# Second-half key and query projections beside the banded attention, value and gate projections in the first DeltaNet phase, and filler work ranked first

## The chip, the cores and the metric

One NeuronCore of a Trainium2 chip runs the whole kernel. The metric is the device time of one execution in microseconds (us), the median of several runs. PE is TensorE (its weight loads are PEld), DVE is VectorE, ACT is ScalarE, POOL is GpSimd, SP is SyncE, whose queue issues most loads from DRAM.

## What is computed

One encoder layer, applied with the same weights to two sequences: a prompt of 512 rows and a sample of 256, each row 1024 wide, all in float32. Tokens are held as six tiles of 128 rows (0 to 3 prompt, 4 and 5 sample).

```python
def _layer(x, mem, ...):
    h = _rms_norm(x, g_pre_mix)
    proj = h @ w_in
    att = _window_attention(aq, ak, av, attn_sink)      # 8 heads, 2 key/value heads, blocks of 128, sink
    dn = _deltanet(qkv, z, ...)                         # 4 heads of 128, conv of 5 taps, both directions
    mix = jnp.concatenate([att, dn], -1) @ w_out
    x = x + _rms_norm(mix, g_post_mix)
    h = _rms_norm(x, g_pre_xa)
    x = x + _rms_norm(_cross_attention(h, mem, xa_wq, xa_wkv, xa_wo, mem_g), g_post_xa)
    h = _rms_norm(x, g_pre_mlp)
    x = x + _rms_norm(jnp.square(jax.nn.relu(h @ w1)) @ w2, g_post_mlp)
    return x
```

The gated DeltaNet takes queries, keys and values through a convolution over time and a SiLU, solves a triangular system in each chunk of tokens, and scans the chunks forward and backward; its output is normed and multiplied by the SiLU of the gate z. The cross-attention's keys and values come from 256 memory rows for each sequence (`mn @ wkv`, 512 columns of keys, 512 of values).

## The kernel before

**Products.** Every large float32 product is made of three matmuls on rounded halves: an operand x becomes hi, a rounded copy made by ACT, and lo, the rest x - hi made by DVE or POOL; hi*hi, hi*lo and lo*hi are added up in PSUM (`mm3`, lines 186 to 190).

**Weights.** `Weights` (lines 82 to 114) holds the units in the order in which they are planned. `get(key, ahead)` calls `emit`, which issues, up to some units ahead of the one wanted, a load on SP into a `raw` tile (line 107; two buffers), the ACT copy to hi (line 108) and the subtraction to lo (line 109). In the first part hi and lo have four buffers each. Which engine subtracts is a function of the key (line 207): POOL for the attention's weights and for the first-half DeltaNet blocks, DVE for the rest.

**What orders the work.** The kernel is traced by generators. `run` and `chain` go through them one after another, `merge` takes steps from two in a given ratio. The framework then writes each engine's instruction order at build time: an instruction that was traced earlier ranks higher, and a later one is put ahead where, by the framework's own timing, the earlier ones are not ready. So a generator that is chained behind another is filler for it. On the chip each engine keeps to its written order. Tiles of one tag share that tag's buffers, in traced order.

**Stages.** `run` (line 193) first norms and transposes the rows and projects the attention's heads (`proj_first`, `proj_att`). Then `merge` interleaves the banded attention (`window`, weight 150) with `proj_dn` for half 0, that is heads 0 and 1 (weight 48, line 220). `proj_dn` (line 539) makes keys, queries and values (kinds 1, 0, 2) of two heads each: six blocks. A block is `feature_major` (line 495): 8 steps of three pairs of matmuls, 512 columns (line 505) and 256 (line 506), into two PSUM banks of one tag; then ACT copies the banks into a padded buffer (lines 549, 550), the convolution runs as one ACT and four DVE steps (lines 554 to 557), a tanh and a DVE product follow, and six transposes (line 568).

Then two DeltaNet phases run, one for each half (`deltanet`, line 658). Each has `prep` (Gram matrices, decays), `inverse`, whose loop of small dependent DVE products (lines 735 and 739) inverts 32-row blocks and is followed by block products on PE, and a scan over the token tiles (`step`). Behind the first phase stands `proj_dn` for half 1 (six blocks), behind the second `fill` (line 276): two of the four memory tiles (`memory_prep`), gate blocks z 0 to 2 (`proj_z`), two more memory tiles, z 3, and the memory's keys and values (`memory_kv`, eight blocks of 128 columns; the four value blocks are transposed afterwards, line 408).

`memory_prep` squares and scales a memory tile on ACT, transposes it in two halves of four, through the tags `tr` (one bank) and `mm` (two banks), and writes hi on ACT (line 388) and lo on DVE (line 389). hi lies in the buffer of half 0's keys, queries and values, so it can be written only when the first phase has read them. The memory rows have two buffers.

Then `tail` makes the output projection, the cross-attention and, while these last, the first part of the MLP for the sample tiles (`up`, line 265, one bank); the MLP follows.

## Time and profile before

| | |
|---|---|
| median of 3 runs | 1214.59 us (1214.43 to 1216.47) |
| profiled execution, its own time | 1215.08 us |
| its span, first to last instruction | 1213.3 us |
| PE busy in the span | 1120.0 us, 92% |
| DVE, ACT, POOL busy | 708.1, 529.4, 355.5 us |
| mean granted TensorE clock | 0.963 of 2.4 GHz |

Times in the profile count from the span's start. A row of waits names the line and tile that waited, then what released it. In the clock column 1.00 is 2.4 GHz and 0.50 is 1.2 GHz. By the timeline the banded attention runs from 94 to 223, the first DeltaNet phase from 223 to 347 (prep to 250, loop to 283, block products to 304, scan), the second from there to 449 (prep to 362, loop to 387, block products to 413, scan), the rest of the memory's keys and values to 497, the tail to about 720.

### The profile page before, as it was taken

The numbers are of one execution on the slowest core, as the hardware profiler recorded it, in microseconds if no ns is written. First come the engines' busy times: TensorE is split into PE (matmuls) and PEld (weight loads), VectorE is DVE, ScalarE is ACT, GpSimd is POOL, SyncE is SP. The second block draws the span as 40 slices with busy tenths as digits, with TensorE's granted clock in tenths as the row PEclk, the third lists the DMA queues.
The fourth block names the chain that finished last, engine by engine and source line by source line (L and its number), as shares of the span: only waits on it lengthen the run. The fifth ranks groups of instructions, "written<-read, shape, count | busy, mean of one in ns | idle before, by whom it ended". The sixth has DMA issues, their size and how long they took to land.

```text
span 1213.3 us, 17783 instructions
## 1 busy us (share of the span) xinstructions
PE 1120.0 (92%) x6800; PEld 958.7 (79%) x6800; DVE 708.1 (58%) x1263; ACT 529.4 (44%) x1119; POOL 355.5 (29%) x415
## 2 busy tenths in 40 slices
PE   6998999976959998899899989999999999999995
PEld 5887888865857887678787778888888888888884
DVE  5313455799789452455535646365658565658656
ACT  5336767755474333433434534443233332333322
POOL 5353210011111020011100136353536353526461
PEclk9999999988989698899899999999999999999998
DMA  6355311211312028732622233122212222212114
GB/s 199 98 180 160 94 53 37 78 35 36 75 48 92 28 93 253 239 122 82 231 70 70 88 122 96 43 75 65 88 53 76 63 70 70 87 52 61 44 57 169
DMA packets 108703, 113.81 MB, mean 94 GB/s; under 512 B 10079, under 2 KB 81867, under 8 KB 108619
## 3 DMA queue, kind: packets, MB, share of 16 engines
q1 hardware_dynamic: 100971, 99.55, 27.3%
q10 hardware_dynamic: 7648, 13.13, 2.9%
q8 instruction: 53, 0.87, 0.3%
q14 instruction: 31, 0.25, 0.1%
HBM read 91.27 MB, written 21.39 MB: 93 GB/s over the span
## 4 chain that ended last, share of the span: by engine, by line
PE 42%; issue 3%; POOL 2%; DVE 2%; DMA 1%; ACT 1%; POOLq 0%; DVEq 0%; ACTq 0%
PE up L1195 7%; PE up L1196 7%; PE up L1197 7%; PE y L189 5%; PE y L188 5%; PE y L190 5%; POOL y L1257 1%; DMA raw<-in_xa_wo 1%; PE xa L1156 1%; PE xa L1137 1%; PE mm L1121 1%; PE mm L1120 1%; PE mm L1119 1%; POOL rs L153 1%; PE mm L188 0%
## 5 line engine op out<-in xcount | busy, mean ns | idle before, releaser
L1200 POOL TENSOR_TENSOR hid<-hid 128x256 f32<-128x256 f32 (+1 forms) x64 | 61.1, 955 | 220.3 <-ACT hid L1199 220.3
L190 PE MATMUL y<-w,hl 128*128 128x512 f32 x318 | 123.8, 389 | 0.5 <-DVE hl L184 0.5
L189 PE MATMUL y<-w,hh 128*128 128x512 f32 x318 | 123.7, 389 | 0.0
L188 PE MATMUL y<-w,hh 128*128 128x512 f32 x318 | 123.7, 389 | 0.0
L1239 DVE TENSOR_TENSOR y<-y,y 128x512 f32<-128x512 f32 x72 | 48.9, 683 | 106.8 <-PE y L190 106.8
L1199 ACT ACTIVATE hid<-up 128x256 f32<-128x256 f32 (+1 forms) x64 | 31.2, 488 | 174.3 <-PE up L1197 174.3
L1195 PE MATMUL up<-hx0h,w 128*128 128x512 f32 x256 | 100.0, 390 | 1.0 <-DVE hx0l L184 1.0
L1196 PE MATMUL up<-hx0l,w 128*128 128x512 f32 x256 | 99.9, 390 | 0.0
L1197 PE MATMUL up<-hx0h,w 128*128 128x512 f32 x256 | 99.6, 389 | 0.0
L109 DVE TENSOR_TENSOR w<-raw,w 128x1024 fp32r<-128x1024 f32 (+1 forms) x58 | 78.8, 1365 | 31.4 <-ACT w L108 31.4
L997 POOL TENSOR_TENSOR quad<-quad 128x1024 f32<-128x1024 f32 x28 | 77.7, 2774 | 33.8 <-DVE w L109 20.2
L109 DVE TENSOR_TENSOR w<-quad,w 128x1024 fp32r<-128x1024 f32 x49 | 73.2, 1505 | 11.9 <-ACT w L108 11.9
L1195 PE MATMUL up<-hx4h,w 128*128 128x256 f32 x256 | 72.2, 282 | 4.2 <-ACT hid L1199 4.2
L1196 PE MATMUL up<-hx4l,w 128*128 128x256 f32 x256 | 71.7, 280 | 0.1
L1197 PE MATMUL up<-hx4h,w 128*128 128x256 f32 x256 | 71.4, 279 | 0.0
L108 ACT ACTIVATE w<-raw 128x1024 fp32r<-128x1024 f32 (+1 forms) x58 | 55.3, 963 | 35.7 <-DMA raw<-in_w_out 11.0
L190 PEld LDWEIGHTS y<-w,hl 128*128 128x128 f32 x318 | 59.7, 188 | 13.3 <-DVE hl L184 0.9
L189 PEld LDWEIGHTS y<-w,hh 128*128 128x128 f32 x318 | 59.7, 188 | 12.4
L188 PEld LDWEIGHTS y<-w,hh 128*128 128x128 f32 x318 | 59.7, 188 | 12.4
L183 ACT ACTIVATE hh<-hid 128x768 fp32r<-128x768 f32 x37 | 31.4, 848 | 83.2 <-PE y L189 64.0
L184 DVE TENSOR_TENSOR hl<-hid,hh 128x768 fp32r<-128x768 f32 x37 | 43.0, 1162 | 24.8 <-ACT hh L183 24.6
L1195 PEld LDWEIGHTS up<-hx0h,w 128*128 128x128 f32 x256 | 48.1, 188 | 10.4 <-DVE hx0l L184 1.2
(373 smaller groups left out, 3114.5 us busy)
## 6 DMA issues: line engine op xcount, KB each, us to landing
raw<-in_mlp_w SPq DMA_DIRECT2D x36, 512.0 KB, 4.5
quad<-in_mlp_w SPq DMA_DIRECT2D x28, 512.0 KB, 4.6
raw<-in_w_in SPq DMA_DIRECT2D x44, 256.0 KB, 3.0
d_x<-x ACTq DMA_DIRECT2D x12, 512.0 KB, 2.6
x<-d_x SPq DMA_DIRECT2D x12, 512.0 KB, 3.7
x<-in_x_prompt SPq DMA_DIRECT2D x8, 512.0 KB, 4.0
raw<-in_xa_wkv SPq DMA_DIRECT2D x16, 256.0 KB, 3.2
d_att<-parts SPq DMA_DIRECT2D x12, 256.0 KB, 2.0
```

The lines of the kernel that those rows point to most:

```text
L108: self.nc.scalar.activation(hi[:, c], raw, AF.Copy)
L109: self.sub(key)(out=lo[:, c], in0=raw, in1=hi[:, c].bitcast(F32), op=ALU.subtract)
L184: nc.vector.tensor_tensor(out=lo, in0=src, in1=hi.bitcast(F32), op=ALU.subtract)
L188: nc.tensor.matmul(ps, lh, rh, start=first, stop=False)
L189: nc.tensor.matmul(ps, lh, rl, start=False, stop=False)
L190: nc.tensor.matmul(ps, ll, rh, start=False, stop=last)
L997: nc.gpsimd.tensor_tensor(out=out, in0=x, in1=y, op=ALU.subtract)
L1195: nc.tensor.matmul(ps, wh[:, k], hh[:, k], start=k == 0, stop=False)
L1196: nc.tensor.matmul(ps, wh[:, k], hl[:, k], start=False, stop=False)
L1197: nc.tensor.matmul(ps, wl[:, k], hh[:, k], start=False, stop=k == 7)
L1200: nc.gpsimd.tensor_tensor(out=r, in0=r, in1=r, op=ALU.mult)
L1239: nc.vector.tensor_tensor(out=y, in0=y, in1=ps, op=ALU.add)
```

## The change

The half-1 keys and queries are chained behind half 0's six blocks and interleaved with the attention (weight 80 for 48). `proj_dn` for half 1 behind the first phase has values alone, and the four z blocks follow it. `fill` keeps `memory_prep` and `memory_kv`. The memory's values are made with the memory rows as the stationary operand, eight units of 128 rows by 512 columns into four banks at once, so they need no transposes. The low parts of half 1's keys and queries go to POOL. `emit`, the transposes and writes of `memory_prep`, and ACT's copies of finished banks in `proj_dn` and `proj_z` are traced inside `high_priority()`, which ranks them ahead of everything else. The first `up` takes the tags `up` and `mm` in turn.

```diff
 class Weights:
     def emit(self, upto):
+        with self.tc.high_priority():
+            self.emit_now(upto)
+
+    def emit_now(self, upto):
         while self.n < min(upto, len(self.q)):
...
 def run(self):
-                         (wp, 512, 2), lambda key: self.nc.gpsimd if key[0] in ("att", "ba") or key[0] == "dn" and key[2] < 2 else self.nc.vector)
+                         (wp, 512, 2), lambda key: self.nc.gpsimd if key[0] in ("att", "ba") or key[0] == "dn" and (key[2] < 2 or key[1] < 2) else self.nc.vector)
...
-        run(merge((self.proj_dn(cv, 0, keep0, ("mm", "dnp")), 48), (self.window(at), 150)))
+        early = chain(self.proj_dn(cv, 0, keep0, ("mm", "dnp")), self.proj_dn(cv, 1, keep1, ("mm", "dnp"), (1, 0)))
+        run(merge((early, 80), (self.window(at), 150)))
...
-        run(self.deltanet(dn, 0, keep0), self.proj_dn(cv, 1, keep1, ("mm", "wn")))
+        run(self.deltanet(dn, 0, keep0), self.proj_dn(cv, 1, keep1, ("mm", "wn"), (2,)), *(self.proj_z(cv, h) for h in range(4)))
...
-        self.up(0, 4, first, "up", 0)
+        self.up(0, 4, first, ("up", "mm"), 0)
...
 def fill(self, pool, m0, keep):
-        prep = self.memory_prep(m0, hh, hl)
-        next(prep)
-        next(prep)
-        yield from self.proj_z(pool, 0)
-        yield from self.proj_z(pool, 1)
-        yield from self.proj_z(pool, 2)
-        next(prep)
-        next(prep)
-        yield from self.proj_z(pool, 3)
+        yield from self.memory_prep(m0, hh, hl)
         yield from self.memory_kv(pool, hh, hl)
...
 def plan_m(self):
-        for m in range(8):
+        for m in range(4):
             for k in range(2):
                 self.W.plan(("kv", m, k), wkv[:, 4 * k:4 * k + 4, m * P:(m + 1) * P], 4, P)
+        for k in range(8):
+            self.W.plan(("v", k), wkv[:, k:k + 1, 512:1024], 1, 512)
...
 def memory_prep(self, m0, hh, hl):
             nc.scalar.activation(x, x, AF.Copy, scale=r)
+            hp = self.tc.high_priority()
+            hp.__enter__()
             for b in (0, 4):
...
+            hp.__exit__(None, None, None)
             yield
...
 def memory_kv(self, pool, hh, hl):
-        for m in range(8):
+        for m in range(4):
...
-            if m < 4:
-                nc.scalar.dma_start(self.d_kT[m], t)
-            else:
-                pt = self.ps("tr")
-                for i in range(4):
-                    nc.tensor.transpose(pt[:, i * P:(i + 1) * P], t[:, i * P:(i + 1) * P], self.ident)
-                v = pool.tile([P, 770], F32, tag="tanh", bufs=1, name="kvv")[:, :512].rearrange("p (i d) -> p i d", i=4)
-                nc.scalar.activation(v, pt.rearrange("p (i d) -> p i d", i=4), AF.Copy)
-                c = (m - 4) * P
-                nc.scalar.dma_start(self.d_v[:, :, c:c + P].rearrange("i p d -> p i d"), v)
+            nc.scalar.dma_start(self.d_kT[m], t)
+
+        pv = [self.ps(("mm", "wn")[i % 2], "mv") for i in range(4)]
+        for k in range(8):
+            wh, wl = self.W.get(("v", k), 3)
+            for i in range(4):
+                c = slice(i * P, (i + 1) * P)
+                self.mm3(pv[i], hh[:, k, c], hl[k // 4][:, k % 4, c], wh[:, 0], wl[:, 0], k == 0, k == 7)
+                yield
+        for i in range(4):
+            v = pool.tile([P, 770], F32, tag="y", bufs=2, name="kvv")[:, :512]
+            nc.scalar.activation(v, pv[i], AF.Copy)
+            nc.scalar.dma_start(self.d_v[i], v)
...
 def proj_z(self, pool, h):
-            nc.scalar.activation(z[:, c], ps, AF.Copy)
+            with self.tc.high_priority():
+                nc.scalar.activation(z[:, c], ps, AF.Copy)
...
-    def proj_dn(self, pool, half, keep, tags):
+    def proj_dn(self, pool, half, keep, tags, kinds=(1, 0, 2)):
-        for kind in (1, 0, 2):
+        for kind in kinds:
...
-                nc.scalar.activation(xp[:, 2:514], pp, AF.Copy)
-                nc.scalar.activation(xp[:, 516:772], psa, AF.Copy)
+                with self.tc.high_priority():
+                    nc.scalar.activation(xp[:, 2:514], pp, AF.Copy)
+                    nc.scalar.activation(xp[:, 516:772], psa, AF.Copy)
...
 def up(self, b, s0, R, tag, ahead=3, ms=range(4)):
-            ps = self.ps(tag, "up")[:, :n]
+            ps = self.ps(tag if isinstance(tag, str) else tag[m % len(tag)], "up")[:, :n]
```

## Rows read from the trace of the kernel before

**Rows 1.** The page, part 1: busy us (share of span) xcount.

```profile
PE 1120.0 (92%) x6800; PEld 958.7 (79%) x6800; DVE 708.1 (58%) x1263; ACT 529.4 (44%) x1119; POOL 355.5 (29%) x415
```

**Rows 2.** Windows by stage: length, busy us (x) of engines, PEclk, DMA.

```profile
94.00:223.00 129.00, 122.34 (x838) 107.33 (x838) 64.85 (x168) 88.86 (x229) 22.99 (x35) 0.99 0.27 77
223.00:250.00 27.00, 22.01 (x139) 19.39 (x137) 21.79 (x47) 18.84 (x47) 0.00 (x0) 1.00 0.30 79
250.00:283.00 33.00, 22.42 (x112) 18.79 (x113) 32.28 (x126) 13.46 (x41) 8.61 (x7) 0.82 0.14 35
283.00:304.00 21.00, 19.92 (x377) 16.31 (x377) 19.50 (x28) 15.05 (x36) 2.33 (x4) 0.88 0.18 48
304.00:347.00 43.00, 40.70 (x313) 36.50 (x308) 32.01 (x88) 20.62 (x70) 9.15 (x18) 1.00 0.29 72
347.00:362.00 15.00, 5.80 (x38) 4.85 (x38) 13.93 (x28) 14.78 (x39) 0.26 (x2) 0.81 0.14 42
362.00:387.00 25.00, 21.39 (x112) 18.13 (x113) 23.62 (x121) 10.79 (x24) 1.43 (x3) 0.84 0.29 91
387.00:413.00 26.00, 23.45 (x364) 19.41 (x362) 16.61 (x32) 13.46 (x29) 2.32 (x4) 0.70 0.13 42
413.00:449.00 36.00, 35.46 (x255) 32.09 (x255) 18.30 (x56) 12.14 (x34) 5.98 (x12) 0.93 0.17 56
449.00:497.00 48.00, 41.74 (x177) 33.01 (x176) 14.43 (x23) 18.91 (x38) 2.03 (x4) 0.92 0.76 231
```

**Rows 3.** Waits of PE from 223 to 497: us in total, times, longest.

```profile
PE mm L505 <- DVE wlo L109: 15.2, 2, 8.5
PE tp L384 <- DVE hm L389: 12.2, 1, 12.2
```

**Rows 4.** Timeline of PE near 365: start, us, operation [idle before <-releaser].

```profile
365.19 1.11 PE L384 MATMUL tp<-ident,xm 128*128 128x128 f32 x4 [12.25 <-DVE hm L389]
...
370.06 0.39 PE L505 MATMUL mm<-hh,whi 128*128 128x512 f32 x1
...
371.10 0.39 PE L505 MATMUL mm<-hh,whi 128*128 128x512 f32 x1
```

**Rows 5.** Windows of line 505: length, PE busy (x), PEld busy (x), PEclk, DMA.

```profile
0.00:94.00 94.00, 5.40 (x15) 2.81 (x15) 1.00 0.51 161
94.00:223.00 129.00, 55.61 (x143) 27.44 (x143) 0.99 0.27 77
```

**Rows 6.** Groups of DVE, 250 to 283: count, busy us, mean ns, idle.

```profile
L735 DVE TENSOR_TENSOR t<-A 128x130 f32<-128x130 f32 (+36 forms) x52 | 11.3, 248 | 0.0
...
L556 DVE SCALAR_TENSOR_TENSOR y<-stage,cw,y 128x770 f32<-128x770 f32 x10 | 10.1, 1008 | 0.5 <-ACT y L554 0.5
L109 DVE TENSOR_TENSOR wlo<-raw,whi 128x512 fp32r<-128x512 f32 x6 | 4.1, 683 | 0.0
```

**Rows 7.** Groups of DVE, 362 to 387: the same columns.

```profile
L389 DVE SCALAR_TENSOR_TENSOR hm<-tp,mgain,hm 128x128 fp32r<-128x128 f32 x8 | 2.8, 344 | 0.4 <-ACT hm L388 0.4
```

**Rows 8.** Lines 388 and 375: ns min/median/max, first and last start.

```profile
L388 ACT ACTIVATE hm<-tp,mgain x32: 342/367/378, 336.1 to 412.3; 128x128 fp32r<-128x128 f32 x32
...
L375 SPq DMA_DIRECT2D xm<-in_mem_sample x2: 328/330/333, 349.8 to 366.3; - x2
```

**Rows 9.** Line 109, GpSimd: ns min/median/max, first and last start.

```profile
L109 POOL TENSOR_TENSOR wlo<-raw,whi x25: 463/1287/2251, 10.0 to 167.3; 128x512 fp32r<-128x512 f32 x24, 128x128 fp32r<-128x128 f32 x1
```

**Rows 10.** Group of PE, 449 to 497: columns as in rows 6.

```profile
L408 PE MATMUL tr<-ident,kvo 128*128 128x128 f32 x16 | 3.1, 323 | 4.9 <-ACT kvo L402 4.9
```

**Rows 11.** The page, part 6: DMA issues, KB each, us to landing.

```profile
d_x<-x ACTq DMA_DIRECT2D x12, 512.0 KB, 2.6
x<-d_x SPq DMA_DIRECT2D x12, 512.0 KB, 3.7
```

**Rows 12.** Waits of PE, 497 to 720.

```profile
PE up L1195 <- ACT hid L1199: 4.2, 3, 2.9
```

**Rows 13.** Waits of PE, 0 to 100.

```profile
PE tp L178 <- DVE h L169: 10.5, 2, 8.0
```

More of the change, by code (lines that the diff above doesn't have):

```diff
@@ L82, with __init__ @@
 class Weights:
-    def __init__(self, nc, new, raw, lo):
+    def __init__(self, tc, nc, new, raw, lo):
+        self.tc = tc
         self.nc, self.new, self.raw = nc, new, raw
@@ L205, in run @@
         wp, g_w = self.open("wB", side="left")
-        self.W = Weights(self.nc, lambda kk, n: [wp.tile([P, kk, n], F32R, tag=x, bufs=4, name="w" + x) for x in ("hi", "lo")],
-                         (wp, 512, 2), lambda key: self.nc.gpsimd if key[0] in ("att", "ba") or key[0] == "dn" and key[2] < 2 else self.nc.vector)
+        self.W = Weights(self.tc, self.nc, lambda kk, n: [wp.tile([P, kk, n], F32R, tag=x, bufs=4, name="w" + x) for x in ("hi", "lo")],
+                         (wp, 512, 2), lambda key: self.nc.gpsimd if key[0] in ("att", "ba") or key[0] == "dn" and (key[2] < 2 or key[1] < 2) else self.nc.vector)
         self.plan_b()
@@ L240, in run @@
         unit.n = 0
-        self.W = Weights(self.nc, unit, (wp, 512, 2), lambda key: self.nc.vector)
+        self.W = Weights(self.tc, self.nc, unit, (wp, 512, 2), lambda key: self.nc.vector)
         self.plan_c()
```

## The prediction

> **What bounds the kernel now.** The page's first part comes first: TensorE (PE) is busy 1120.0 of 1213.3 us [rows 1], so time can come from PE's idle stretches, from its low clock, or from less PE work; little work is removed here. The windows by stage say where the lost time lies [rows 2]. From 94 to 223 the banded attention and the first half's projections keep PE at 122.34 of 129: bound by PE. The two DeltaNet phases are not: 250 to 283 has PE at 22.42 of 33 with DVE at 32.28, and 347 to 362 has PE at 5.80 of 15 with DVE at 13.93 and ACT at 14.78. There the chain prep, inverse loop, block products, scan sets the length and the projections are only filler. From 449 to 497 nothing is left but memory keys and values, a tail of 48 us with PE alone at work. PE's waits name two places where filler existed but PE could not have it: 15.2 us on a weight's low part (L109) that stood in DVE's queue behind the inverse, and 12.2 us on the memory tiles' low part (L389) [rows 3]. In the timeline the z block on the mm banks starts only after the second wait, at 365 [rows 4]: both mm banks were held by memory tiles that nobody emptied. After each wait the clock row is under 1: 0.82, 0.88, 0.81, 0.84, 0.70 [rows 2]; at these means part of each stretch ran at 1.2 instead of 2.4 GHz.
>
> **The change part by part**, against the profiled execution's own 1215.1 us (0.5 above the median shown, 1214.6).
>
> *Window stage, 129 us.* Four blocks (two K, two Q) of 24 pairs of matmuls (512 and 256 columns) move in. Three pairs take 1.04 us from start to start [rows 4], so a pair is 0.347. 15 + 143 of L505 had run by 223 and the first half has 144 [rows 5], so 14 of the 96 pairs were here already: 82 x 0.347 = 28.5, and 24 transposes at about 0.15 (four in 0.6) = 3.6. Stage +32. It stays PE's: ACT's 88.86 us carries six blocks and the attention, so four more cost at most 4/6 of it, 59, which makes 148 of 161; DVE by the same bound 108. The evacuation is ranked first now, which can only shorten the wait for a bank. The eight low parts that go to GpSimd cost 8 x 1.287 = 10.3 us [rows 9] beside 22.99 of 129 busy [rows 2]; what is queued behind them there is the attention's small sum (L952), for which DVE waits. I take 0, bounds -2 and +5. The eight weight loads on SP stand before query loads that are fetched a tile ahead; 0, in the same bounds. GpSimd's low part spreads from 463 to 2251 ns [rows 9], so something holds it up. The Trainium skill, "SBUF — State Buffer", section "SBUF: two separate sides", says that GpSimd and a DVE instruction with two SBUF inputs share a port pair under an exclusive lock. By that rule the stage would be longer by up to 8 x 2.25 = 18 us if DVE set its length; by the rows DVE has that room, and I stay at 0.
>
> *First DeltaNet phase, 124 us (223 to 347).* Its filler was six blocks with convolutions (less the 14 pairs), and is now two value blocks and four z blocks: 144 pairs for 130 or so, the same PE work, about 97 to 105 us (the stages' busy sum 105.1, less at most 8.4 for the clock under 1). What leaves is DVE work out of the chain's queue: the loop of 33 us held ten convolution steps of about 1 us and six low parts of 0.68 [rows 6]; its own products have the other 18 or so. With one value block (five steps) and eight low parts left in it I take 27: -6. The convolutions that leave prep and copies give -3, those that leave the scan -3 (estimates: three steps each). The 15.2 us of waits go because low parts now rank ahead of the inverse; what is late next is the chain itself. Phase -12; bounds 0 (DVE order unchanged) and -24 (PE never waits).
>
> *Second phase, 150 us (347 to 497).* The z blocks (33 us of PE) are gone; memory preparation and 192 matmuls of keys and values remain. Prep: memory tiles rank first, 32 ACT steps of 0.367 and as many DVE steps of 0.344 [rows 7, 8], of which the prep stretch held few before; some 20 more on either engine, overlapping, put +5 on it. They cannot start before the first half's tiles are read out: same buffer. Loop: 13 memory steps leave it, -4. Block products: 26 us at clock 0.70 against 21 at 0.88 in the first phase [rows 2], -5. Scan 36: 0. Then the tail: keys and values (192 matmuls of 512 columns, two thirds of a pair each, 0.23: 44 us) fit beside loop, products and scan, 83 us with some 35 of DeltaNet's own, so after the scan only the round trip of the mixed rows is left, 2.6 + 3.7 to land [rows 11] and about 3 of norm: 9 for 48, -39. This also hides the 16 transposes of values, 3.1 busy and 4.9 of waits [rows 10], now removed. Phase -43; bounds -58 (PE never waits) and -5 (rival 1).
>
> *Elsewhere.* The second bank for the early MLP tiles can save the 4.2 us of waits [rows 12], but its mm tiles come after the cross-attention's own: -2. At the start weight loads and splits rank ahead of the rows x and their norms, where PE waits 10.5 us already [rows 13]: +2, bounds 0 and +4. High rank in the tail and in the MLP, where PE is the bound: 0, bounds -3 and +3.
>
> Sum: +32 - 12 - 43 - 2 + 2 = -23, so 1215.1 - 23 = 1192, and 1191.6 by the median: **1192**.
>
> **The rivals.**
> 1. *Memory tiles late; slower.* Before, their writes ran from 336.1 to 412.3 [rows 8], past the loop's end, and the last two loads left SP only at 349.8 and 366.3, each after an earlier tile was transposed. If rank does not mend that, there is no filler at all in the second phase's prep and loop, now that z is gone: PE has 57 us after the loop, 35 of them DeltaNet's, for 44 of keys and values; 22 remain after the scan (13 more than the round trip) and 10 are added by the low clock after an empty loop. 1192 + 23 = 1215; with ACT and DVE steps of 11 us ahead of the chain's prep, only 5 of which I counted, 1221. It decides if the last memory write comes after the loop. For it: that row. Against: z, which came between the tiles in rank, is out of the way.
> 2. *A cold back half.* After waits the clock rows fall [rows 2], and 387 to 413, small block products with little filler, is at 0.70. In the first phase the new filler can run out before products and scan (21 + 43 = 64 us). If a quarter of that stretch is chain matmuls that take twice as long at 1.2 GHz (my estimate; at most 40.70 of 43 is PE at all), 16 are added, less what short spells cost: 1204 to 1212. The Trainium skill, "TensorE: Matmul & The Clock Gate", section "HAM oscillation — how this bites in real kernels", says that bursts of matmuls with gaps between start throttled again each time; by that rule this rival is the outcome, with the rows at 365 and at 387 agreeing.
> 3. *PE becomes the bound again.* If the chain hides wholly, the first phase takes PE's 98 and the second 83 + 9: -14 and -15 more, 1163 to 1178. For it: window stage, where filler is dense. Against: the chain's own lengths.
> 4. *Filler only changes places.* If idle and clock losses stay as large, only the transposes and 4.9 us of waits are saved: 1207 to 1215.
>
> **How the numbers follow.** Forecast (1178 to 1204) 0.50; rival 1 0.14; rival 2 0.16; rival 3 0.12; rival 4 0.08, more than half of it within 0.2% (2.4 us, about what a measurement here tells from no change). So faster 0.81, same 0.05, slower 0.14. The range goes from 1168, in the middle of rival 3, to 1214: it leaves out the slow rival and the far end of the third, 0.2.
>
> **What would show it.** Right: K and Q blocks of the second half (L505 on mm and dnp) inside a window stage that ends near 255; the 15.2 and 12.2 us waits gone; last L388 and L389 before the second loop ends; kv matmuls done by the scan's end and out-tile transposes near 474. Wrong: PE idle over 15 us in the second prep and loop (rival 1), clock rows under 0.8 in the first scan (rival 2), or a window stage over 170 us.

## The result, and the profile after

The changed kernel takes 1249.94 us (median of 4 runs, 1244.95 to 1252.34) against 1214.51 us for the kernel before in the same session: a ratio of 1.0286 (95% interval 1.0253 to 1.032). It is 35 us slower, where 23 less were forecast, and lies outside the range. Its profiled execution has a span of 1248.4 us, 35.1 more than the profiled execution before.

First the page's part 1, as [rows 1]:

```profile
PE 1133.3 (91%) x6784; PEld 969.5 (78%) x6784; DVE 713.2 (57%) x1255; ACT 528.1 (42%) x1115; POOL 373.6 (30%) x423
```

PE runs 16 instructions fewer (the transposes of the values) and is busy 13 us longer. The same matmuls take more time, so part of the loss is clock.

The windows by stage are cut as in [rows 2], except that a loop's window runs here to the first block product, 2 to 3 us past the loop's last step, and there to about that step (length; busy us and instructions of PE, PEld, DVE, ACT, POOL; granted clock; DMA share and GB/s):

```profile
97.00:249.00 152.00, 147.05 (x991) 128.71 (x990) 77.03 (x183) 106.05 (x280) 42.10 (x51) 1.00 0.27 77
249.00:285.00 36.00, 35.55 (x220) 30.76 (x219) 31.41 (x61) 26.35 (x75) 0.30 (x1) 1.00 0.34 95
285.00:318.00 33.00, 29.53 (x160) 25.16 (x158) 30.52 (x120) 12.39 (x29) 0.75 (x2) 0.90 0.34 107
318.00:338.00 20.00, 15.04 (x331) 13.66 (x332) 10.08 (x17) 9.76 (x16) 2.33 (x4) 0.68 0.11 38
338.00:380.00 42.00, 31.84 (x215) 29.37 (x215) 21.75 (x76) 12.71 (x42) 6.45 (x13) 0.83 0.15 46
380.00:400.00 20.00, 8.82 (x55) 7.55 (x53) 18.58 (x44) 18.51 (x56) 2.16 (x5) 0.84 0.15 51
400.00:431.00 31.00, 28.31 (x115) 22.87 (x115) 29.07 (x124) 10.76 (x21) 0.58 (x2) 0.89 0.33 98
431.00:454.00 23.00, 19.92 (x340) 15.75 (x341) 10.99 (x17) 9.05 (x14) 2.78 (x4) 0.72 0.10 30
454.00:499.00 45.00, 42.92 (x274) 37.06 (x272) 24.35 (x66) 18.61 (x46) 6.32 (x12) 0.91 0.28 88
499.00:516.00 17.00, 0.82 (x4) 0.82 (x5) 3.67 (x5) 4.21 (x11) 1.78 (x4) 0.61 0.95 323
```

From 249 to 318 PE is as full as was meant (65.08 of 69 us). From 318 it is not: block products and first scan have PE at 46.88 of 62 us and the clock at 0.68 and 0.83, where they had 0.88 and 1.00 before. The last matmul of the filler (values and z) ends at 322. And from 499 to 516 PE does next to nothing.

PE's waits in the two phases, as [rows 3] (total us, times, longest):

```profile
PE tp L183 <- DMA b<-d_mix: 16.5, 1, 16.5
PE tp L386 <- ACT xm L380: 8.0, 1, 8.0
```

The 15.2 us on a low part are gone, as forecast, and of the 12.2 us on hm 2.3 are left. The new first row, 16.5 us, is for the mixed rows: the results of attention and DeltaNet, which are written to DRAM and loaded again by the tail. The memory tiles are written from 375 to 407, as their line shows (compare [rows 8]):

```profile
L390 ACT ACTIVATE hm<-tp,mgain x32: 357/367/423, 375.2 to 406.5; 128x128 fp32r<-128x128 f32 x32
```

The last surprise is the MLP. PE's waits from 727 to 1199, then two windows of that stretch:

```profile
PE y L193 <- DVE y L1247: 8.1, 4, 2.0
PE y L193 <- DVE yc L1247: 3.1, 1, 3.1
```

```profile
727.00:800.00 73.00, 69.53 (x325) 58.29 (x326) 32.96 (x25) 25.96 (x38) 37.60 (x20) 0.95 0.33 101
...
900.00:1000.00 100.00, 95.94 (x484) 81.39 (x483) 56.81 (x61) 31.98 (x41) 37.96 (x22) 0.97 0.19 58
```

Before, the MLP (713 to 1164) had PE at 450.70 of 451 us and no such wait. Now it takes 472.

A table by events says where the time went. The attention's last matmul, half 0's last scan step, the first transpose of the gate of an out tile (a token tile of the output projection, with which the tail opens; line 1085 after) and the end of the span cut the execution in four; the numbers are starts or ends in each run's trace, and the medians and ratios are those of its timed runs. The experiments are in it already, numbered as they were run: the fourth run is e4.

| run | median us | ratio (95%) | attention ends | first scan ends | out tiles begin | span |
|---|---|---|---|---|---|---|
| before | 1214.51 | 1 | 223.1 | 339.2 | 497.8 | 1213.3 |
| after | 1249.94 | 1.0286 (1.0253 to 1.032) | 248.9 | 378.9 | 516.1 | 1248.4 |
| e1 rank in first list only | 1229.4 | 1.0119 (1.0075 to 1.0163) | 248.2 | 377.5 | 513.4 | 1227.4 |
| e2 before + weights' rank | 1238.12 | 1.0182 (1.0127 to 1.0238) | 220.9 | 354.6 | 504.1 | 1239.4 |
| e3 before + order | 1237.49 | 1.0175 (1.0126 to 1.0224) | 247.4 | 370.6 | 520.5 | 1235.4 |
| e4 after, no weights' rank | 1215.16 | 1.0007 (0.9978 to 1.0035) | 250.3 | 374.0 | 490.9 | 1210.8 |
| e5 e4, only keys early | 1208.34 | 0.9925 (0.9895 to 0.9955) | 232.9 | 359.6 | 489.8 | 1205.1 |
| e6 e5, last z block late | 1210.35 | 0.9954 (0.9931 to 0.9978) | 232.3 | 361.9 | 483.0 | 1208.6 |
| e7 e4, no memory rank | 1241.01 | 1.0194 (1.0161 to 1.0227) | 250.4 | 374.6 | 512.0 | 1239.1 |
| e8 e4 + low parts of second list ranked | 1232.71 | 1.0127 (1.0095 to 1.0158) | 251.9 | 373.0 | 492.1 | 1230.3 |
| e9 e5, low parts on GpSimd | 1206.29 | 0.994 (0.9916 to 0.9964) | 232.4 | 363.0 | 488.3 | 1204.8 |
| e10 e9 + mixed rows ranked | 1207.03 | 0.9936 (0.9912 to 0.9961) | 231.2 | 361.7 | 480.4 | 1203.6 |
| e11 e4 + memory weights ranked | 1229.74 | 1.0131 (1.0085 to 1.0177) | 251.1 | 377.7 | 513.9 | 1227.7 |
| e12 e4, old value blocks | 1216.33 | 1.0027 (1.0002 to 1.0052) | 250.2 | 371.4 | 493.8 | 1214.4 |
| e13 e10 + whole memory tile ranked | 1198.34 | 0.9905 (0.987 to 0.994) | 227.8 | 361.3 | 489.6 | 1203.9 |
| e14 e4 + warming matmuls | 1212.0 | 0.9987 (0.9956 to 1.0017) | 251.4 | 368.0 | 490.7 | 1204.8 |
| e15 e5 + mixed rows and whole memory tile ranked | 1198.6 | 0.9891 (0.986 to 0.9922) | 228.5 | 356.2 | 480.7 | 1198.0 |

After against before, stage by stage: +25.8 to the attention's end, +13.9 in the first phase, -21.4 from there to the out tiles, +16.8 in tail, MLP and finish; together the 35.1.

### The profile page after: what moved, and what is told of

It is laid out like the page before. It is cut to its first block, busy times and chain, and to the rows that moved or that the text cites. A ratio compares the mean times of both kernels' runs of the same rounds, so it can differ in the third digit from the quotient of the medians.

```text
span 1248.4 us, 17780 instructions
## 1 busy us (share of the span) xinstructions
PE 1133.3 (91%) x6784; PEld 969.5 (78%) x6784; DVE 713.2 (57%) x1255; ACT 528.1 (42%) x1115; POOL 373.6 (30%) x423
## 4 chain that ended last, share of the span: by engine, by line
PE 40%; DVE 4%; issue 4%; POOL 2%; ACT 1%; DMA 1%; DVEq 0%; POOLq 0%; ACTq 0%
PE up L1203 7%; PE up L1204 7%; PE up L1205 7%; PE y L193 5%; PE y L195 5%; PE y L194 5%; DVE w L114 2%; POOL y L1265 1%; DMA raw<-in_xa_wo 1%; ACT w L113 1%; PE xa L1164 1%; PE xa L1145 1%; PE mm L1129 1%; PE mm L1128 1%; PE mm L1127 1%
## 5 line engine op out<-in xcount | busy, mean ns | idle before, releaser
L193 PE MATMUL y<-w,hh 128*128 128x512 f32 x318 | 126.7, 398 | 11.2 <-DVE y L1247 8.1
L1208 POOL TENSOR_TENSOR hid<-hid 128x256 f32<-128x256 f32 (+1 forms) x64 | 71.6, 1121 | 196.5 <-ACT hid L1207 196.5
L195 PE MATMUL y<-w,hl 128*128 128x512 f32 x318 | 126.5, 398 | 0.5 <-DVE hl L189 0.5
L194 PE MATMUL y<-w,hh 128*128 128x512 f32 x318 | 126.2, 397 | 0.0
L114 DVE TENSOR_TENSOR w<-quad,w 128x1024 fp32r<-128x1024 f32 x49 | 86.2, 1768 | 68.5 <-ACT w L113 68.5
L114 DVE TENSOR_TENSOR w<-raw,w 128x1024 fp32r<-128x1024 f32 (+1 forms) x58 | 71.0, 1233 | 18.9 <-ACT w L113 18.8
L113 ACT ACTIVATE w<-quad 128x1024 fp32r<-128x1024 f32 x49 | 50.8, 1049 | 51.8 <-PE up L1205 45.8
L195 PEld LDWEIGHTS y<-w,hl 128*128 128x128 f32 x318 | 61.0, 192 | 13.9 <-DVE hl L189 0.9
L189 DVE TENSOR_TENSOR hl<-hid,hh 128x768 fp32r<-128x768 f32 x37 | 47.6, 1288 | 33.9 <-ACT hh L188 33.7
## 6 DMA issues: line engine op xcount, KB each, us to landing
raw<-in_mlp_w SPq DMA_DIRECT2D x36, 512.0 KB, 4.5
quad<-in_mlp_w SPq DMA_DIRECT2D x28, 512.0 KB, 4.0
d_x<-x ACTq DMA_DIRECT2D x12, 512.0 KB, 2.6
x<-d_x SPq DMA_DIRECT2D x12, 512.0 KB, 3.8
x<-in_x_prompt SPq DMA_DIRECT2D x8, 512.0 KB, 5.1
```

The lines of the kernel that those rows point to most:

```text
L113: self.nc.scalar.activation(hi[:, c], raw, AF.Copy)
L114: self.sub(key)(out=lo[:, c], in0=raw, in1=hi[:, c].bitcast(F32), op=ALU.subtract)
L189: nc.vector.tensor_tensor(out=lo, in0=src, in1=hi.bitcast(F32), op=ALU.subtract)
L193: nc.tensor.matmul(ps, lh, rh, start=first, stop=False)
L194: nc.tensor.matmul(ps, lh, rl, start=False, stop=False)
L195: nc.tensor.matmul(ps, ll, rh, start=False, stop=last)
```

## The experiments

**What the weights' rank does, and where (e1 to e4).** The weights are held in two lists: the first for projections and memory, the second for output, cross-attention and MLP. e1 keeps the rank for the first alone:

```diff
     def emit(self, upto):
+        if not self.ranked:
+            return self.emit_now(upto)
         with self.tc.high_priority():
             self.emit_now(upto)
...
-        self.W = Weights(self.tc, self.nc, unit, (wp, 512, 2), lambda key: self.nc.vector)
+        self.W = Weights(self.tc, self.nc, unit, (wp, 512, 2), lambda key: self.nc.vector, False)
```

> The changed kernel with the weights' rank kept for the first list of weights (up to the second DeltaNet phase) and taken from the second list (output projection, cross-attention, MLP). Theory A (rank costs in the MLP: the low parts, ranked first on DVE, delay the adds L1247 that empty the y banks, and on SP the loads of the output weights hold the mixed rows' load back): the MLP stage goes back from 472 to about 451, the 8.1 and 4.0 us of PE waits on L1247 go, the hole of 16.5 us after the second scan shrinks to about 10; 1250 - 20 - 6 = about 1224. Rival B (the MLP is longer because of the second up bank, or because of what the earlier stages leave behind): the time stays at 1245 to 1252. Rival C (the order of the filler costs it all): within 3 us of 1250 as well, with the MLP at 470.

1229.4 us, with out tiles to end at 714.0 in place of 732.3. So the rank of the second list costs 18 to 21 us, as theory A had it. The hole before the out tiles, PE's wait for the mixed rows, did not shrink, though (16.05 us in its trace): that part of A fell, and e11 takes it up.

e2 is the kernel before with the rank alone (`emit` as in the change, nothing else).

> The kernel before with one edit alone: weights' loads and splits at high rank, everywhere. Theory A: about +20 in the MLP, +3.5 at the start, and the 15.2 us wait for a low part in the first DeltaNet phase goes (-5 to -15 there): 1214.5 + 24 - 10 = about 1228 (1220 to 1240). Rival C (the rank is harmless, the order costs): 1200 to 1215, with the MLP at 451.

1238.12: the rank costs 24 us by itself, 19.8 of them behind the out tiles' start. It gained nothing in the first phase, which grew from 116.1 to 133.7 us, where I had expected 5 to 15 less: the wait for low parts is gone from its trace, but PE waits 11.2 us for ACT to empty banks instead, and the DVE loop takes 38.3 us in place of 33.5.

e3 is the kernel before with the order alone:

```diff
-        run(merge((self.proj_dn(cv, 0, keep0, ("mm", "dnp")), 48), (self.window(at), 150)))
+        early = chain(self.proj_dn(cv, 0, keep0, ("mm", "dnp")), self.proj_dn(cv, 1, keep1, ("mm", "dnp"), (1, 0)))
+        run(merge((early, 80), (self.window(at), 150)))
...
-        run(self.deltanet(dn, 0, keep0), self.proj_dn(cv, 1, keep1, ("mm", "wn")))
+        run(self.deltanet(dn, 0, keep0), self.proj_dn(cv, 1, keep1, ("mm", "wn"), (2,)), *(self.proj_z(cv, h) for h in range(4)))
```

> The kernel before with the order alone: second half's K and Q projected in the window stage (with their low parts on GpSimd as in the change), V and the four z blocks in the first DeltaNet phase, memory alone in the second; no rank, value blocks and up bank as before. Theory A with the order neutral: 1200 to 1220, MLP at 451, start of the window stage at 94. Rival C (the order costs by itself: no filler at the back of either phase, cold clock, no cover for the mixed rows' round trip): 1225 to 1250.

1237.49: the order, too, costs 23 us by itself. Its trace has the memory tiles written from 366.0 to 433.8, and PE at 13.90 of 46 us from 370 to 416. That is rival 1's mechanism. e4 takes the weights' rank out of the change altogether:

```diff
     def emit(self, upto):
-        with self.tc.high_priority():
-            self.emit_now(upto)
+        self.emit_now(upto)
```

> The changed kernel with the weights' rank taken out everywhere (all other ranks, the value blocks and the second up bank stay). Theory A: MLP at 451, window stage starts at 94, 1214 to 1224, the same as the run with the rank in the first list only or up to 10 faster (start, and loads on SP that stand ahead of DeltaNet's); longer than that one by up to 10 if the wait for low parts behind the inverse (15 us before) comes back. Rival C: 1240 to 1250.

1215.16, the same as before. So what the order costs, the other parts of the change give back (e7 shows which), and the whole 35 us of the change is the weights' rank: some 20 in the second list (after against e1) and 14 in the first (e1 against e4).

**Which part of the rank: low parts (e8).** e4 with only the subtractions of the second list ranked:

```diff
-                self.sub(key)(out=lo[:, c], in0=raw, in1=hi[:, c].bitcast(F32), op=ALU.subtract)
+                hp = self.tc.high_priority() if self.ranked else nullcontext()
+                with hp:
+                    self.sub(key)(out=lo[:, c], in0=raw, in1=hi[:, c].bitcast(F32), op=ALU.subtract)
```

> The fourth run's kernel (change without the weights' rank) with only the low parts of the second list of weights (output, cross-attention, MLP) ranked first; their loads and their high parts (ACT) keep their places. Theory A (it is the low part, ahead of the adds that empty the y banks in DVE's queue): nearly all of the 20 us come back, 1230 to 1237, MLP stage at 465 to 472. Rival F (it is the loads on SP or the high parts on ACT): 1213 to 1220.

1232.71, with 738.2 us from the out tiles to the end against e4's 719.9: the low parts on DVE are enough. PE's wait in that run's MLP:

```profile
PE y L195 <- DVE y L1249: 11.4, 4, 4.1
```

How they do it stands in DVE's groups of the MLP (columns: busy us, mean ns of one, then idle time just before them and what ended it), first after, then before:

```profile
L114 DVE TENSOR_TENSOR w<-quad,w 128x1024 fp32r<-128x1024 f32 x49 | 86.2, 1768 | 68.5 <-ACT w L113 68.5
...
L1247 DVE TENSOR_TENSOR y<-y,y 128x512 f32<-128x512 f32 x69 | 45.8, 683 | 61.1 <-PE y L195 61.0
```

```profile
L109 DVE TENSOR_TENSOR w<-quad,w 128x1024 fp32r<-128x1024 f32 x49 | 73.2, 1505 | 11.9 <-ACT w L108 11.9
...
L1239 DVE TENSOR_TENSOR y<-y,y 128x512 f32<-128x512 f32 x69 | 46.9, 683 | 103.2 <-PE y L190 103.2
```

Ranked first, a low part is written into DVE's queue as soon as the framework thinks it ready, ahead of the add that empties a y bank (a PSUM bank of the MLP's second product). On the chip DVE then stands still for ACT's high part (68.5 us in place of 11.9), and the add behind it finds its product ready more often (it waits 61.0 us for PE in place of 103.2). DVE in the changed kernel's first place where PE waits for a bank:

```profile
765.65 2.31 DVE L114 TENSOR_TENSOR w<-quad,w 128x1024 fp32r<-128x1024 f32 x1 [0.48 <-ACT w L113]
767.89 1.63 DVE L114 TENSOR_TENSOR w<-raw,w 128x1024 fp32r<-128x1024 f32 x1
769.45 2.06 DVE L114 TENSOR_TENSOR w<-quad,w 128x1024 fp32r<-128x1024 f32 x1
771.43 1.87 DVE L1247 TENSOR_TENSOR yc<-yc,y 128x512 f32<-128x512 f32 x3
```

Three low parts in a row go first, then three adds at once. All five places look like that, with 5.7 to 5.9 us of low parts ahead of the adds; in the four later ones DVE also waits 6.0 to 7.8 us for ACT before them. But the wait for ACT is not what it takes: in e8, where the high parts kept their place, DVE does not wait for ACT at any of the four places, and three low parts in a row (5.7 to 8.3 us) are enough. One of them:

```profile
919.89 5.55 DVE L116 TENSOR_TENSOR w<-quad,w 128x1024 fp32r<-128x1024 f32 x2
925.36 2.82 DVE L116 TENSOR_TENSOR w<-raw,w 128x1024 fp32r<-128x1024 f32 x1
928.10 1.27 DVE L1249 TENSOR_TENSOR y<-y,y 128x512 f32<-128x512 f32 x2
```

In the changed kernel PE's waits sum to 11.2 us, and its busy time in the stage grows from 450.70 to 460.40 us for the same matmuls, at a clock of 0.95 to 0.98 in the windows with waits: together the 21 us by which the stage is longer.

**Which weights of the first list (e11).** e4 with the rank for the 16 memory weights alone (the keys `kv` and `v` in `emit_now`):

```diff
+            hp = self.tc.high_priority() if key[0] in ("kv", "v") else nullcontext()
+            hp.__enter__()
...
+            hp.__exit__(None, None, None)
```

> The fourth run's kernel (change without the weights' rank, 1215.2) with high rank for the 16 weights of memory keys and values alone. In the run with the whole first list ranked (1229.4) the second phase was 19 us longer than in the fourth. Theory I (those weights' splits, ahead of the chain's DVE and ACT steps, lengthen the loop and leave PE cold behind it): 1222 to 1232. Rival J (what the first phase and the start hand on): 1213 to 1218.

1229.74, all that the whole first list costs (e1, 1229.4). Theory I holds. From the first scan's end to the out tiles it takes 136.2 us, against 116.9 in e4. Three windows of e11, after its second loop:

```profile
430.00:440.00 10.00, 6.97 (x246) 5.59 (x246) 6.40 (x9) 7.24 (x10) 2.78 (x4) 1.00 0.11 40
440.00:460.00 20.00, 19.93 (x131) 16.35 (x132) 5.44 (x11) 2.38 (x5) 0.00 (x0) 0.51 0.05 15
460.00:490.00 30.00, 28.72 (x204) 25.96 (x204) 18.09 (x54) 13.29 (x35) 6.12 (x12) 0.99 0.23 76
```

Eight low parts in place of e4's three went into its second prep and loop (5.5 us of DVE, and 0.7 of waiting for ACT), and the block products began at 430.1 against 423.1; 3.7 of these 7 us come from the later end of its first scan. PE then works 19.93 of 20 us, but at 1.2 GHz, which gives some 10 us away (an estimate: half of them); from the first block product to the last scan step it takes 62.5 us, against 51.1 in e4. The keys and values ended at 496.6, 4 us behind the last scan step; in e4 they ran on for 14 us behind it and covered most of the mixed rows' round trip. So PE waits 16.4 us for them, much as in e1 and after. SP has a part in that: in the changed kernel it issued the load only at 509.17, 11.5 us after the last scan step, behind weight loads, one of which had itself waited 6.5 us for the write of the mixed rows. Of the 19 us, 6 come back behind the out tiles' start (713.8 us from there to the end, e4 719.9).

**What the order needs: the memory tiles' rank (e7).** e4 without it:

```diff
-            hp = self.tc.high_priority()
-            hp.__enter__()
...
-            hp.__exit__(None, None, None)
```

> The fourth run's kernel (change without the weights' rank) with the memory tiles' high rank taken out as well. Theory (memory tiles late, as in the run with the order alone, where PE idled 30 of the 28 + 20 us before the second block products): the last memory write comes some 20 us later, after the second loop; 1215 + 15 to 22 = 1230 to 1237, like the order alone. Rival (the order alone lost its 23 us to the value blocks, the one up bank or the unranked evacuations): 1213 to 1220.

1241.01, 26 more than e4 and a little over what was expected. PE's waits from 374 to 445 and its windows:

```profile
PE dnp L769 <- DVE C L746: 16.0, 1, 16.0
PE tp L383 <- DVE hm L388: 14.2, 3, 8.9
```

```profile
374.00:404.00 30.00, 13.36 (x67) 11.09 (x66) 26.04 (x77) 21.46 (x62) 2.74 (x6) 0.67 0.11 36
404.00:420.00 16.00, 0.57 (x16) 0.50 (x16) 16.00 (x83) 2.42 (x6) 0.00 (x0) 0.50 0.00 1
420.00:447.00 27.00, 23.66 (x350) 19.61 (x347) 11.56 (x24) 9.74 (x19) 2.33 (x4) 0.50 0.01 2
```

The whole second loop passes without filler and the products behind it run at 1.2 GHz. With e3 this shows rival 1's late memory tiles as the price of the order when that rank is missing. Between e3 and e7 lie the ranked copies of banks, the value blocks and the second up bank: 1.0175 and 1.0194, with intervals that overlap, so these three together are worth nothing that can be seen here.

**The value blocks (e12).** e4 with the memory values as before (`memory_kv` and `plan_m` of the kernel before).

> The fourth run's kernel (1215.2) with the memory values as before: four feature blocks, their transposes and copies in place of token blocks. By the prediction's price the 16 transposes are hidden beside the second scan, or cost up to 8.0 us (3.1 busy and 4.9 of waits) where they are not: 1215 to 1223. Rival (the token blocks, which hold four banks at once, cost more than they save): 1208 to 1214.

1216.33 against 1215.16: the ratios' intervals overlap, so no difference is shown, and in any case not the 8 us of the upper bound.

**How much order (e5, e6).** Queries back into the first phase:

```diff
-        ... self.proj_dn(cv, 1, keep1, ("mm", "dnp"), (1, 0)))
-        run(merge((early, 80), (self.window(at), 150)))
+        ... self.proj_dn(cv, 1, keep1, ("mm", "dnp"), (1,)))
+        run(merge((early, 64), (self.window(at), 150)))
...
-        run(self.deltanet(dn, 0, keep0), self.proj_dn(cv, 1, keep1, ("mm", "wn"), (2,)), ...
+        run(self.deltanet(dn, 0, keep0), self.proj_dn(cv, 1, keep1, ("mm", "wn"), (0, 2)), ...
```

> The changed kernel without the weights' rank (the fourth run, 1215.2), and with one change of order: of the second half only the keys are projected in the window stage; queries, values and the four z blocks are the first DeltaNet phase's filler (8 blocks in place of 6). Theory D (the order takes filler from the first phase's back half, which then runs with gaps and at the low clock): window stage 16 shorter (two blocks at 8.3), the first phase about as long as it was (125, the filler now reaching past the block products), so 1215 - 10 = 1205 (1199 to 1209), the clock row of the first scan nearer to 1. Rival E (PE's queue makes the phase longer by what is put into it): the phase grows by the same 16 and the time stays at 1213 to 1217.

1208.34, 0.7% under the kernel before, with an interval clear of 1. Its attention ends 17.4 us sooner than e4's and its first phase is 3 us longer, not 17: the filler went into time that was idle. What is left of PE's waits in the two phases is again the low part behind the inverse:

```profile
PE mm L510 <- DVE wlo L113: 12.1, 2, 9.6
PE mv L193 <- DVE wlo L113: 6.8, 1, 6.8
```

> As the run before (only keys early), and the last z block moved from the first phase to the second, between the memory tiles and the memory keys. Theory D: the second phase's prep, where PE idles for some 16 us beside low clock, takes the block for nothing, or it covers the mixed rows' round trip: 2 to 6 below the run before, if that one's first phase is bound by PE; equal to it within 3 if its first phase is bound by the chain. Rival E: equal within 2.

e6 moves the last z block behind the memory tiles: 1210.35, equal to e5 within the intervals. Its out tiles begin 6.8 us sooner, and the stretch behind them is 10.3 longer. Most of that is one wait: once the mixed rows are transposed, PE waits 8.3 us for ACT's high part of them (1.0 in e5). e10 shows the same wait.

**Low parts on another engine (e9, e10).** e5 with all low parts of the first list on GpSimd:

```diff
-  ... lambda key: self.nc.gpsimd if key[0] in ("att", "ba") or key[0] == "dn" and (key[2] < 2 or key[1] < 2) else self.nc.vector)
+  ... lambda key: self.nc.gpsimd)
```

> The fifth run's kernel (no weights' rank, only the keys early; 1208.3) with all low parts of the first list of weights made on GpSimd. Theory G (what is left of the wait that the rank was to cure is a low part behind the inverse in DVE's queue: 2.4 and 9.6 us at 263 and 284, 6.8 us at 410, each with low clock behind it, 10.2 + 20.5 and 13.7 us): the 19 us of waits go, and some 10 of clock loss, part of which comes back as an earlier end of the filler: 1190 to 1200. Rival H (GpSimd's low parts, 1.3 to 2.3 us each, hold DVE up or come later than DVE's did): 1205 to 1220.

1206.29: both waits are gone, others stand in their place (6.5 and 7.4 us for the loops' results), and next to nothing is gained. In the first prep and loop DVE's own products became slower. First e5 (233 to 300), then e9 (232 to 309):

```profile
L742 DVE TENSOR_TENSOR t<-A 128x130 f32<-128x130 f32 (+36 forms) x52 | 11.4, 253 | 0.0
```

```profile
L742 DVE TENSOR_TENSOR t<-A 128x130 f32<-128x130 f32 (+36 forms) x52 | 16.7, 352 | 0.0
```

The same 52 products take 352 ns each in place of 253 while GpSimd makes 13 low parts of 1917 ns (one in e5), and from the attention's end to the first block product it takes 76 us against e5's 67. In e9's trace the 22 of the 52 that run beside such a low part take 510 ns in the mean and the other 30 take 237. Of the 9 us some 7 are the loop's own products (this line and the line of its adds, 254 to 290 ns each); the rest is three convolution steps more in the loop and a microsecond of idle time, less the six low parts that left it. Rival H holds. The Trainium skill, "SBUF — State Buffer", section "SBUF: two separate sides", says that GpSimd and a DVE instruction with two SBUF inputs exclude each other on a shared port pair: here the trace agrees, 253 to 352 ns, in a stretch where DVE does set the length.

e10 ranks the first two loads of mixed rows:

```diff
-        nc.sync.dma_start(mix, self.d_mix[t])
+        hp = self.tc.high_priority() if t > 3 else nullcontext()
+        with hp:
+            nc.sync.dma_start(mix, self.d_mix[t])
```

> As the run before, with high rank for the two loads of mixed rows of the sample tiles, which open the tail. Theory: the hole of 13.8 us after the second scan is a load that stands on SP behind weight loads at DMA share 0.98; ranked first it lands within 3.7 us, so 5 to 9 less than the run before. Rival (the wait is for the write of the rows and the transfers in flight, not for a place in SP's queue): within 2 of the run before, or longer, as SP then waits for the mixed rows ahead of the weight loads.

1207.03: the out tiles begin 7.9 us sooner than in e9 and the time is the same. That is the rival's outcome but not its reason, since a place in SP's queue did bring the rows sooner. What is lost comes right behind. First PE's longest wait from 478 on, then ACT in front of it:

```profile
PE mm L193 <- ACT hx4h L188: 7.9, 2, 7.7
```

```profile
487.02 0.60 ACT L417 ACTIVATE kvv<-mv 128x512 f32<-128x512 f32 x1 [2.90 <-DMA d_v<-kvv]
488.02 0.60 ACT L188 ACTIVATE hx4h<-tp 128x512 fp32r<-128x512 f32 x1 [0.40 <-ACT kvv L417]
```

The high part of the transposed rows stands in ACT's queue behind the copies of the memory's value banks, which share two buffers, so that each waits until an earlier one is written to DRAM. Rows that come late do not meet this (e9's are transposed at 487.4), rows that come early do (e10's at 479.9). Ranking these copies or giving them more buffers was not tried.

**The low clock in the first scan (e14).** e4 with 96 matmuls added behind the z blocks, products that nobody reads:

```diff
+    def warm(self, n):
+        for i in range(n):
+            ps = self.ps("wn", "warm")
+            for k in range(8):
+                self.nc.tensor.matmul(ps, self.hh[:, k, 0:P], self.hh[:, k, 0:512], start=k == 0, stop=k == 7)
+            yield
...
-  ... *(self.proj_z(cv, h) for h in range(4)))
+  ... *(self.proj_z(cv, h) for h in range(4)), self.warm(12))
```

> The fourth run's kernel (change without the weights' rank, 1215.2) with 96 matmuls of 512 columns added behind the z blocks in the first phase, whose products nobody reads (20.5 us at full clock by 0.213 each). In the fourth run PE is idle for some 10 us from 320 to 375 and at the low clock for 17.1 + 6.8. Theory K (the low clock lengthens block products and scan, so that rival 2 is the step that failed): with PE warm the chain from the first block product to the last scan step is 5 to 12 us shorter, 1204 to 1211. Rival L (the chain's length is set by DVE and ACT between its matmuls): that stretch stays within 3 us of 60, and the time at 1213 to 1220, or rises with what the added matmuls take from the chain (up to 1228).

Two windows each, prep and loop, then products and scan; first e4, then e14:

```profile
250.00:314.40 64.40, 61.40 (x375) 53.07 (x374) 60.20 (x179) 37.05 (x102) 1.02 (x3) 1.00 0.35 101
314.40:374.00 59.60, 46.29 (x543) 42.31 (x543) 32.09 (x90) 23.11 (x57) 8.72 (x17) 0.80 0.18 52
```

```profile
251.40:315.60 64.20, 61.16 (x375) 52.81 (x374) 60.28 (x179) 36.95 (x102) 1.02 (x3) 1.00 0.36 100
315.60:368.00 52.40, 49.19 (x600) 42.69 (x601) 32.34 (x92) 23.61 (x59) 8.68 (x17) 1.00 0.19 59
```

The same chain takes 52.4 us at clock 1.00 and 59.6 at 0.80, so theory K holds in that stretch. Its whole time shows no gain (1212.0, runs from 1204.79 to 1219.09, ratio 0.9987 with 1 inside the interval), and the out tiles begin where they did: its first scan ends 6.0 us sooner than e4's, its second 0.9, and then PE waits for the mixed rows.

**Two last ranks (e13, e15).** The whole work of a memory tile is ranked, not its transposes alone, since the third tile's square stood on ACT behind the second phase's prep; e13 is on top of e10, e15 on top of e5 (with e10's rank of the mixed rows):

```diff
+            hp = self.tc.high_priority()
+            hp.__enter__()
             nc.scalar.activation(junk, x, AF.Square, accum_out=ss)
             r = self.rsqrt(m0, ss, 1, 1.0 / D, EPS, "rs1")
             nc.scalar.activation(x, x, AF.Copy, scale=r)
-            hp = self.tc.high_priority()
-            hp.__enter__()
             for b in (0, 4):
```

> The tenth run's kernel (only keys early, low parts on GpSimd, mixed rows ranked; 1207.0) with the high rank taken over the whole of a memory tile's work (square, root, scaling, and transposes as before). Theory: the 8.5 us wait of PE at 380, where the third tile's square stands behind the second phase's prep on ACT, goes, and 3 to 5 of clock loss behind it: 1196 to 1203. Rival: the filler is then used up sooner and PE waits in the loop or for the mixed rows instead: 1204 to 1209.

> The fifth run's kernel (only keys early, no weights' rank, low parts as in the change; 1208.3) with high rank for the sample tiles' mixed rows and over the whole memory tile. Its memory tiles were not waited for (1.5 us), but PE waited 13.8 us for mixed rows: -3 to -6 by the latter alone, 1202 to 1206. Rival (the tail takes it back, as in the sixth run, whose out tiles began 7 us sooner and ended no sooner): 1207 to 1210.

1198.34 and 1198.6, the first inside what was expected and the second better, and the fastest of the study: e15's ratio is 0.9891 (0.986 to 0.9922), 1.1% under the kernel before. What PE still waits for in e15's phases:

```profile
PE mm L511 <- DVE wlo L114: 11.6, 2, 9.7
PE tp L183 <- DMA b<-d_mix: 8.1, 1, 8.1
PE mv L194 <- DVE wlo L114: 6.5, 1, 6.5
```

The hole before the out tiles is 8.1 us in place of e5's 13.8, and the stretch behind it took back 2.0. That is not the whole gain: of the 9.1 us by which its out tiles begin sooner than e5's, 4.4 are there when the attention ends, a stage that neither rank was meant for (by then 9 fewer of the projections' matmuls are done, and the clock from 94 to 150 is 1.00 in place of 0.97). What each of the two ranks gives was not separated. e13's profiled execution has a span of 1203.9, above its own median, so its trace is not used to explain its gain.

## Why the prediction was wrong

Against its terms the change came out at -8 us in window stage and start, +26 in the first phase, +22 in the second and +19 behind the out tiles' start: together the 58 between -23 and +35.

**The step that failed outright, a term put at nothing,** is the last sentence of the part "Elsewhere": "High rank in the tail and in the MLP, where PE is the bound: 0, bounds -3 and +3." It measured +18 to +21 (after against e1, and e8 against e4). PE was the bound with 0.3 us of slack in 451, and I read that as nothing else can matter. It means the opposite: every instruction of DVE that empties a bank is due at a fixed time, and a rank that puts others before it shows in full. No rival held this; the one slow outcome was given to the memory tiles alone.

**The second phase**, -43: right in its first half. The memory tiles were all written within 32 us and before the loop's end, the keys and values were done when the scan ended, and the transposes were gone; without the weights' rank the stretch from first scan to out tiles is 41.7 us shorter than before (e4, 116.9 against 158.6), close to the forecast. In the change it is 21.4 shorter: block products and scan, which were to save 5, take 66.7 us in place of 59.5, and from the last scan step to the out tiles it takes 18.4 in place of 49.0, where 39 less were forecast. What was missing is again the rank, of the memory's weights this time (e11): I let it only cure waits. I priced the round trip behind the scan at 9 us; PE's wait in it was 16.5, and it is small only where filler outlasts the scan (e4) or the load is issued sooner (e15). The prediction's 83 us for loop, products and scan count the products at 26 where its own term makes them 21; with 78 us, the 79 of PE work that it puts there would just not have fitted.

**The first phase**, -12, with rank and without: +13.9 after, +7.6 in e4. Two terms failed. The first is prep and copies, forecast at -3. From the attention's end to the first block product it takes 63.9 us before, 64.1 in e4 and 69.4 after, and the loop is not the reason: from its first product to its last it takes 33.5 us before, 29.0 in e4 and 31.1 after, so that most of its -6 came in e4. Prep grew from 27.0 to 33.1 and 36.2. DVE's groups of prep show why, first before (223 to 250), then after (249 to 285):

```profile
L556 DVE SCALAR_TENSOR_TENSOR y<-stage,cw,y 128x770 f32<-128x770 f32 x3 | 3.0, 1005 | 0.0
```

```profile
L564 DVE SCALAR_TENSOR_TENSOR y<-stage,cw,y 128x770 f32<-128x770 f32 x7 | 7.1, 1020 | 1.1 <-ACT y L562 1.1
...
L114 DVE TENSOR_TENSOR wlo<-raw,whi 128x512 fp32r<-128x512 f32 x6 | 4.1, 685 | 2.5 <-ACT whi L113 2.5
```

The same for the loop's window after (285 to 318), beside [rows 6]:

```profile
L564 DVE SCALAR_TENSOR_TENSOR y<-stage,cw,y 128x770 f32<-128x770 f32 x5 | 5.1, 1017 | 0.0
L114 DVE TENSOR_TENSOR wlo<-raw,whi 128x512 fp32r<-128x512 f32 x7 | 4.8, 682 | 2.2 <-ACT whi L113 2.1
```

Five convolution steps left the loop; two products behind the value blocks (1.9 us), a seventh low part and 2.2 us of waiting for ACT came in. Prep had three convolution steps before and has seven after, since the last query block's convolution ran over from the window stage, and six low parts where it had none. So the steps that were to leave prep came into it. The second term is the scan: "-3" was +7.5 in e4 and +8.5 after for block products and scan together, and that is rival 2's mechanism, to which I gave 0.16. e14 shows that it is the clock: with PE kept at work the same stretch is back at 52.4 us, where it was before (52.1). The Trainium skill, "TensorE: Matmul & The Clock Gate", section "HAM oscillation — how this bites in real kernels", has bursts of matmuls between waits start throttled each time; by that rule the scan was to lose time, and the traces of e4 and e14 agree (0.80 and 1.00). With rival 2's own 12 to 20 the first phase would have stood between 0 and +8; that e4's +7.6 lies there is in part luck: of the some 20 us over the forecast, 10.5 are block products and scan, and the rest is prep and loop, of which rival 2 says nothing.

**What held.** Window stage and start, +34: +25.8 to the attention's end, with 467 of the 480 matmuls of its ten blocks done by 249; a little over-priced. PE stayed its bound: its waits there sum to 4.9 us, for 6.5 before, so neither the evacuations, nor GpSimd's low parts, nor the loads on SP show a cost. The start moved by 3.8 us (first matmul at 11.8 in place of 8.0, PE's wait on the first norms 11.8 us in place of 8.0), inside 0 to +4. Rival 1's mechanism and price (+23 to +29 on the forecast) are those of e7, +26 on e4, only that the rank did mend it. The 15.2 and 12.2 us waits went, the first not for the reason given: without the weights' rank e4 has 1.7 us of it left, and the order alone (e3) 6.6. One term beside these did not hold, the second up bank: the wait on hid went from 4.2 to 3.0 us, and the time from out tiles to end (e4 719.9, e1 714.0, before 715.5) shows no gain.

**In sum**: the order was worth about nothing as made (e4), since what the second phase gained went into the window stage and a cold scan. It was worth 7 to 9 us with the queries left in the first phase (e5; by medians and by the ratio) and 13 to 14 with two ranks more (e15).

## What to carry to other kernels

Where an engine writes down its order at build time, a rank is not a help to what is ranked but a loan from everything behind it in the same queue: rank the last short step that someone waits for (a transpose, a copy that frees a buffer), and not producers, of which several will then stand in a row before that step. A stage in which one engine is busy all the time is, here, where a rank on another engine's queue is dearest. Filler is to be dealt out so that each phase keeps some until its chain ends, and a little past it where a round trip through DRAM follows; filler that is done early costs twice, by the idle time and by the clock of what runs next.

## What the runs showed that was not expected

The low clock outlasts the idle time that precedes it: in e11 PE was at work for 19.93 of 20 us at 0.51, behind ten us in which it had been busy for 6.97, and in e7 the 27 us behind an empty loop ran at 0.50 with PE at 23.66. It does not always follow: in e4 PE was busy for 6.15 and 7.54 us of the 20 from 410 to 430, and the next ten ran at 1.00. The runs do not show what decides.

GpSimd as a way around DVE's queue costs DVE: 99 ns on each of 52 products (253 to 352 ns), and 9 us on prep and loop, some 7 of them by such products, for 12 low parts more.

A load ranked first helped in one setting (e15, a hole of 8.1 us for 13.8) and not in another (e10, 7.9 us sooner and no gain). In e15 the keys and values end at 471.7, before the rows have landed (479.8), and PE's wait for ACT's high part is 2.0 us; in e10 they end at 478.7, and it is 7.7.
